# First loads, norm vectors, and four instruction orders in a two-layer transformer trunk: eight start-up loads in place of twelve

## The chip, the cores and the metric

The kernel runs on one core of one Trainium2 chip. Its time is device microseconds (us) of one launch, from the runs of the unprofiled kernel; lower is better. Everything else comes from one profiled execution. PE is TensorE (matmuls; its weight loads are shown as PEld), ACT is ScalarE, DVE is VectorE, POOL is GpSimd, and SP is the engine that issues most DMAs. A name with q (SPq) is an engine's sequencer.

## The reference

One sequence of 512 tokens with 1024 features goes through two layers, all in fp32. Cut to what matters:

```
for i in range(2):
    hn = rmsnorm(h, norm_mix_g[i])
    h = h + (even_mixer(hn) if i == 0 else odd_mixer(hn))   # projection, attention, output projection
    hn = rmsnorm(h, norm_mlp_g[i])
    h = h + square(relu(hn @ w_mlp_up[i])) @ w_mlp_down[i]   # 1024 -> 4096 -> 1024
    gate = sigmoid(rmsnorm(h, norm_ple_g[i]) @ w_ple_gate[i])
    h = h + (p[i] @ w_ple_proj[i]) * gate
return rmsnorm(h, final_norm_g)
```

Layer 0 mixes 8 stick-breaking heads with 4 differential heads, which need a scalar made of four short lambda vectors; layer 1 has 16 heads of dilated window attention. A relative-position bias table is added to the logits of all softmax heads.

## The kernel before

The state is held transposed: eight tiles h[0] to h[7], each 128 features by 512 tokens. Every fp32 operand of a matmul is split into a high part (ACT rounds it to fp32r: `hi`, `wh`) and the rest (DVE or POOL subtracts: `lo`, `wl`); a product is three matmuls, hi x wh, lo x wh and hi x wl (`mm3`, lines L141, L144, L145). The order on each engine is fixed when the program is built: a scheduler arranges the instructions by their dependencies, and `order(later, earlier)` adds a dependency by hand without a semaphore. Each engine then works strictly in its order. A DMA that SP issues is tied to one of eight completion semaphores in turn, so the ninth waits for the first to land.

Start-up. SP issues twelve loads: the norm vectors (`gcols`), and eight state tiles with the first weight block (the query weights of head group 2) in three pieces between them:

```
chunks = {0: slice(0, 2), 1: slice(2, 4), 3: slice(4, 8)}
nc.sync.dma_start(gcols, gvec)
for k in range(KT):
    nc.sync.dma_start(h[k], xT[k])
    if k in chunks:
        nc.sync.dma_start(raw0v[:, :, chunks[k]], src0[:, :, chunks[k]])
```

`raw0` holds the two output halves of the block one after the other, so that a piece of it has two rows per partition. Ten fp32 matmuls on an identity (`warm`, L311) come first on PE. Then the query product runs input tile by input tile (banks `sc`), then the key product (banks `mm`), half by half. `prepare()` (L337 to L359) loads the bias table's parts and the lambda vectors, and makes the bias rows (`urow`) and the lambda scalar (`neglam`). `statistics()` squares the eight state tiles on ACT (L248), adds them on DVE (L261), and `finish` turns the sum into 1/rms: split (L268, L269), two matmuls with a matrix of ones (L270, L271), Ln and Exp on ACT (L213, L216), and three DVE steps (L217 to L219) that give `rstd`. The evacuations of queries (`qq`, L493 to L500), keys (`kh`, `klz`, L509 to L511) and values (`v`, L461, L462) wait for it. The weight tiles `wh` and `wl` have three buffers each.

Attention. A step makes scores (L532, L533), a minimum and exponentials (L549, L552), transposes (L558) and their eviction (`transposed`, L566 and L567: `pth` on ACT, `ptl` on DVE), and later the product with the values (L577). `interleave` weaves these steps into the projection of the next group, or, for the last group, into the output projection `out_first`, which splits the finished head outputs `oT` (`split_tile`, L182, L183) as it needs them.

MLP. Up and down projections run in four chunks of the hidden width; the down product is a seven-product Strassen form on 256-column halves, with weight sums made on DVE (`s13`, `s24`, L797, L800) and split (L809, L810). In the last chunk the side sums are collected by accumulating DMAs from POOL (L835), and `finished(c)` folds them into h (`side_sums`, L920) and splits the new h for the gate projection.

End. `ple_final` turns h to token-major tiles of 128 tokens (`ht`), and for each makes the gate (L1032 to L1034), the sum of squares (L1035), 1/rms and the scaling (`finish`, L983 on ACT and L985 on DVE, then two output DMAs). The last tile uses Ln and Exp for 1/rms, the others an integer start with three Newton steps on DVE (`rsqrt_cols`, L284, L285, L279 to L281).

Of the kernel before, what the change touches and what calls it, by code (L numbers as in the profile page):

```python
# [19 lines left out]
P = 128  # L20
# [12 lines left out]
UL = 640  # L33
WARM = 10
# [28 lines left out]
def trunk(  # L63
    ctx: ExitStack,
    tc: tile.TileContext,
    xT, pT, gvec, t5_table, lambdas, w_in, w_outa, w_outb, w_up, w_down, w_gate, w_proj,
# [111 lines left out]
    def split_tile(src, scale=None, bufs=8):  # L178
        hi = apool.tile([P, S], F32R, tag="hi", name=nm("hi"), bufs=bufs)
        lo = apool.tile([P, S], F32R, tag="lo", name=nm("lo"), bufs=bufs)  # L180
        if scale is None:
            nc.scalar.activation(hi, src, AF.Copy)  # L182
            nc.vector.tensor_tensor(lo, src, hi.bitcast(F32), op=ALU.subtract)  # L183
        else:
            last_split[:] = [nc.scalar.activation(hi, src, AF.Copy, scale=scale).ins]
            nc.vector.scalar_tensor_tensor(lo, src, scale, hi.bitcast(F32), op0=ALU.mult, op1=ALU.subtract)  # L186
        return hi, lo
# [111 lines left out]
    h = [const([P, S], f"h{k}") for k in range(KT)]  # L299
    gcols = const([P, 49], "gcols")  # L300
# [13 lines left out]
    raw0v = raw0.rearrange("p (i k c) -> p i k c", i=2, k=KT)  # L314
    src0 = w_in[0, 0].rearrange("p (i k c) -> p i k c", i=2, k=KT)
    blk0 = [tuple(wpool.tile([P, KT, P], F32R, tag=t, name=nm(t), bufs=3) for t in ("wh", "wl")) for _ in range(2)]
    chunks = {0: slice(0, 2), 1: slice(2, 4), 3: slice(4, 8)}
    nc.sync.dma_start(gcols, gvec)
    for k in range(KT):
        nc.sync.dma_start(h[k], xT[k])  # L320
        if k in chunks:
            nc.sync.dma_start(raw0v[:, :, chunks[k]], src0[:, :, chunks[k]])
    for k in range(KT):
        norm.done(k, stats=False)
        if k in chunks:
            for i, (hi, lo) in enumerate(blk0):
                ck = chunks[k]
                nc.scalar.activation(hi[:, ck], raw0v[:, i, ck], AF.Copy)
                nc.vector.tensor_tensor(lo[:, ck], raw0v[:, i, ck], hi[:, ck].bitcast(F32), op=ALU.subtract)
# [4 lines left out]
    def prepare():  # L334
        a, b, c, d = (mix[0].tile([P, S], F32, tag="bias", name=nm("prep"), bufs=4) for _ in range(4))
        lamt = t2k("tmp")[:, 0:4 * HD].rearrange("p (j c) -> p j c", j=4)
# [9 lines left out]
        for c0, src, offm in ((0, a[0:32], (b[0:16], c[0:16])),  # L346
                              (512, d[0:32, 0:128], (d[0:16, 128:256], d[0:16, 256:384]))):
            up = ps("pv" if c0 == 0 else "tp")[0:16, 0:src.shape[-1]]
            nc.tensor.matmul(up, d[0:32, 384:400], src, start=True, stop=True)
            for l in range(2):  # L350
                nc.vector.scalar_tensor_tensor(offm[l], up, -1.0, offm[l], op0=ALU.mult, op1=ALU.add)
                nc.sync.dma_start(urow[l, :, c0:c0 + src.shape[-1]], offm[l])
        nc.vector.tensor_tensor(lamt[:, 0:2, :], lamt[:, 0:2, :], lamt[:, 2:4, :], op=ALU.mult)
        lsum = const([P, 2], "lsum")
        nc.vector.reduce_sum(lsum, lamt[:, 0:2, :], axis=AX.X)
        nc.scalar.activation(lsum, lsum, AF.Exp)
        nc.vector.tensor_tensor(neglam, lsum[:, 1:2], lsum[:, 0:1], op=ALU.subtract)
        nc.vector.tensor_scalar(neglam, neglam, -LAMBDA_INIT, None, op0=ALU.add)
        nc.vector.tensor_scalar(gsub, gcols[:, 48:49], -0.5 * (D // P) * (1.0 - LAMBDA_INIT), None, op0=ALU.mult)  # L359
# [31 lines left out]
    def mixer(layer, norm, nxt):  # L391
# [31 lines left out]
        first = []  # L423
# [3 lines left out]
        def project(g, cur):  # L427
# [38 lines left out]
            def queries_keys():  # L466
                qscale = -0.5 * HD ** -0.5 if kind == "sb" else 0.5 * HD ** -0.5
                qk, waiting = [], []
                for isq in (True, False):
                    src = next_block()  # L470
                    lo_eng[0] = nc.vector if start else nc.gpsimd
                    blk = blk0 if isq and start and not layer else block(src, KT, P)
                    lo_eng[0] = nc.gpsimd
# [87 lines left out]
        def transposed(tp, i, pt):  # L561
            n = P * (i + 1)
            src = tp[:, 0:n].rearrange("p (j c) -> p j c", c=P)
            dh = pth[pt][:, i:i + 3 * i + 1:3, :]
            dl = ptl[pt][:, i:i + 3 * i + 1:3, :]
            nc.scalar.activation(dh, src, AF.Copy)  # L566
            nc.vector.tensor_tensor(dl, src, dh.bitcast(F32), op=ALU.subtract)  # L567
# [116 lines left out]
        def out_first():  # L684
# [23 lines left out]
        else:  # L708
            interleave(out_first(), 72.0, attend(*cur))
# [20 lines left out]
    def mlp(layer, fpool, norm, nxt):  # L730
# [51 lines left out]
        def down(ch, c):  # L782
# [95 lines left out]
            if last and c:  # L878
                finished(c - 1)
# [28 lines left out]
        def finished(c):  # L908
            side_sums(c, low)
# [56 lines left out]
    def ple_final(layer, fpool, pj, norm):  # L966
# [13 lines left out]
        done = []  # L980

        def finish(t, r, after=()):
            cp = nc.scalar.activation(hk[t][:, 0:512], hk[t][:, 0:512], AF.Copy, scale=r)  # L983
            nc.sync.dma_start(out[0, t * P:(t + 1) * P, 0:512], hk[t][:, 0:512])
            sc = nc.vector.scalar_tensor_tensor(  # L985
                hk[t][:, 512:1024], hk[t][:, 512:1024], r, gb[:, 512:1024], op0=ALU.mult, op1=ALU.mult)
            if after:
                order(cp.ins, after[0].ins)
                order(sc.ins, after[1].ins)
            nc.sync.dma_start(out[0, t * P:(t + 1) * P, 512:1024], hk[t][:, 512:1024])  # L990

        for c in range(2):
# [31 lines left out]
            for t in range(QT):  # L1024
                last = c == 1 and t == QT - 1
                for i, (c0, n) in enumerate(parts[t]):
# [8 lines left out]
                    nc.scalar.activation(gt, hs, AF.Square, accum_out=ssq[t][:, c + i:c + i + 1])  # L1035
# [3 lines left out]
                m, r, w = (spool.tile([P, 1], F32, tag="fin", name=nm("fin"), bufs=6) for _ in range(3))  # L1039
                sq = ssq[t]  # L1040
                nc.vector.tensor_tensor(m, sq[:, 0:1], sq[:, 1:2], op=ALU.add)
                nc.vector.tensor_scalar(m, m, 1.0 / D, NORM_EPS, op0=ALU.mult, op1=ALU.add)
                if last:
                    tables = use_tables([sg.ins])
                    ln = nc.scalar.activation(r, sq[:, 2:3], AF.Ln, scale=1.0 / D, bias=m)
                    order(ln.ins, tables)
                    ex = nc.scalar.activation(r, r, AF.Exp, scale=-0.5)
                    nc.vector.scalar_tensor_tensor(m, sq[:, 2:3], 1.0 / D, m, op0=ALU.mult, op1=ALU.add)
                    newton(r, m, w)
                else:  # L1050
                    rsqrt_cols(r, m, w)
                done.append((t, r))
                if t < QT - 2:
                    finish(*done.pop())
        for t, r in done[::-1]:
            finish(t, r, () if t == QT - 1 else (ex, ad))
# [34 lines left out]
def _feeds(a):  # L1091
# [3 lines left out]
    for layer, w in enumerate((a["w_in_even"][0], a["w_in_odd"][0])):  # L1095
        blocks = []
        for j, g in enumerate(GROUPS[layer]):
# [6 lines left out]
            qk = [_pack(w, all8, c, 256, 2) for c in (q, k)]  # L1104
# [6 lines left out]
    gs = [a[n].reshape(DEPTH * KT, P) for n in ("norm_mix_g", "norm_mlp_g", "norm_ple_g")] + [a["subln_g"]]  # L1111
    onehot, offs = _consts()
    feeds = {
        "xT": a["x"][0].T.reshape(KT, P, S),
        "pT": a["p"][:, 0].transpose(0, 2, 1).reshape(DEPTH, 2, P, S),
        "gvec": np.concatenate(gs, axis=0).T,
# [39 lines left out]
```

## Time and profile before

| what | value |
|---|---|
| median of 3 runs | 1297.12 us (1297.03 to 1297.26) |
| the profiled execution: its own time, its span | 1296.47 us, 1294.7 us |
| PE busy, weight loads busy | 1277.1 us (99%), 1125.5 us (87%) |
| DVE, ACT, POOL busy | 1003.3 us (77%), 710.0 us (55%), 212.5 us (16%) |
| mean granted TensorE clock | 0.997 |
| DMA moved, mean rate | 144.25 MB, 111 GB/s |

The span runs from the first to the last instruction; the execution's own time is 1.8 us longer. Matmuls overlap in the record (a 512-column matmul is shown with 0.39 us, but the next starts 0.23 us later), so a PE that looks busy may still be waiting a few tenths; the start times of successive matmuls tell it.

### The profile page before, as it was taken

What the parts mean: (1) busy time and instruction counts of PE and PEld (TensorE: products, weight loads), DVE (VectorE), ACT (ScalarE), POOL (GpSimd) and SP (SyncE); (2) the same over time, 40 slices, a digit from 0 to 9 for tenths busy, and PEclk for the clock granted to TensorE, in tenths of its full rate; (3) what the DMA queues carried; (4) which work ended last, traced back from release to release, by engine and by line L of the source; (5) the groups of instructions that cost most, each with busy time, mean ns of one, the idle gap of its engine ahead of it and who ended that gap; (6) DMA issues with size and microseconds to landing.
All of it is one profiled execution on the core that took longest, in us unless ns stands there. A gap on an engine that the chain in (4) does not pass through costs nothing.

```text
span 1294.7 us, 19322 instructions
## 1 busy us (share of the span) xinstructions
PE 1277.1 (99%) x7520; PEld 1125.5 (87%) x7520; DVE 1003.3 (77%) x1673; ACT 710.0 (55%) x1149; POOL 212.5 (16%) x184
## 2 busy tenths in 40 slices
PE   9999999999999999999999999999999999999997
PEld 7988887888988989989889888788899898898986
DVE  6788798778858869679767777887785785986976
ACT  6667868555535334356456666765553443534544
POOL 2433433400000000001024333222000000000201
PEclk9999999999999999999999999999999999999998
DMA  6421423222232322647432222212323223255741
GB/s 213 141 82 53 160 74 114 90 98 98 85 112 98 101 99 95 195 110 201 153 128 84 82 90 77 70 58 83 112 98 103 93 98 121 75 153 141 185 165 66
DMA packets 33995, 144.25 MB, mean 111 GB/s; under 512 B 3888, under 2 KB 4624, under 8 KB 21232
## 3 DMA queue, kind: packets, MB, share of 16 engines
q1 hardware_dynamic: 29680, 135.16, 30.7%
q0 software_dynamic: 4224, 7.87, 3.5%
q8 instruction: 59, 0.97, 0.3%
q14 instruction: 32, 0.26, 0.1%
HBM read 131.92 MB, written 6.37 MB: 107 GB/s over the span
## 4 chain that ended last, share of the span: by engine, by line
PE 80%; DVE 10%; ACT 4%; DMA 2%; issue 2%; POOL 0%; SPq 0%; ACTq 0%; DVEq 0%; POOLq 0%
PE mm L141 11%; PE mm L144 11%; PE mm L145 11%; PE sc L144 5%; PE sc L145 5%; PE sc L141 5%; PE pv L145 4%; PE pv L144 4%; PE pv L141 4%; PE tp L145 4%; PE tp L144 4%; PE tp L141 4%; PE pv L577 3%; PE tp L558 2%; PE tp L894 2%
## 5 line engine op out<-in xcount | busy, mean ns | idle before, releaser
L122 ACT ACTIVATE wh<-raw 128x1024 fp32r<-128x1024 f32 (+1 forms) x156 | 160.5, 1034 | 135.4 <-PE mm L144 51.0
L126 POOL TENSOR_TENSOR wl<-raw,wh 128x512 fp32r<-128x512 f32 (+1 forms) x132 | 177.9, 1370 | 303.7 <-ACT wh L122 301.3
L141 PE MATMUL mm<-hi,wh 128*128 128x512 f32 x472 | 187.1, 396 | 0.2 <-ACT pjt L381 0.2
L145 PE MATMUL mm<-hi,wl 128*128 128x512 f32 x472 | 184.8, 391 | 0.1
L144 PE MATMUL mm<-lo,wh 128*128 128x512 f32 x472 | 184.6, 391 | 0.0
L128 DVE TENSOR_TENSOR wl<-raw,wh 128x1024 fp32r<-128x1024 f32 x90 | 109.6, 1222 | 39.6 <-ACT wh L122 34.1
L145 PEld LDWEIGHTS mm<-hi,wl 128*128 128x128 f32 x472 | 88.6, 188 | 20.0 <-POOL wl L126 0.5
L141 PEld LDWEIGHTS mm<-hi,wh 128*128 128x128 f32 x472 | 88.7, 188 | 16.9 <-ACT pjt L381 0.4
L144 PEld LDWEIGHTS mm<-lo,wh 128*128 128x128 f32 x472 | 88.8, 188 | 15.5
L780 POOL DMA_DIRECT2D s<-in_w_down_dram x4 | 4.5, 1123 | 580.0 <-DMA s<-in_w_down_dram 313.7
L809 ACT ACTIVATE wh<-s 128x1024 fp32r<-128x1024 f32 x58 | 61.1, 1053 | 53.0 <-DVE s L796 14.7
L552 ACT ACTIVATE e<-e,mn 128x128 f32<-128x128 f32 (+3 forms) x96 | 53.8, 561 | 62.3 <-DVE mn L549 61.9
L771 DVE TENSOR_TENSOR ul<-u,uh 128x1792 fp32r<-128x1792 f32 x32 | 64.8, 2024 | 29.6 <-ACT uh L770 29.5
L810 DVE TENSOR_TENSOR wl<-s,wh 128x1024 fp32r<-128x1024 f32 x58 | 70.8, 1221 | 12.6 <-ACT wh L809 12.2
L770 ACT ACTIVATE uh<-u 128x1792 fp32r<-128x1792 f32 x32 | 54.5, 1703 | 45.7 <-DVE u L768 45.4
L759 ACT ACTIVATE u<-u 128x512 f32<-128x512 f32 x64 | 39.7, 626 | 68.1 <-DVE u L758 68.1
L144 PE MATMUL sc<-lo,wh 128*128 128x512 f32 x184 | 72.3, 393 | 0.4 <-DVE lo L186 0.4
L141 PE MATMUL sc<-hi,wh 128*128 128x512 f32 x184 | 72.2, 392 | 0.0
L145 PE MATMUL sc<-hi,wl 128*128 128x512 f32 x184 | 71.9, 391 | 0.0
L141 PE MATMUL mm<-wh,hi 128*128 128x256 f32 (+1 forms) x216 | 63.4, 293 | 0.0
L145 PE MATMUL mm<-wh,lo 128*128 128x256 f32 (+1 forms) x216 | 63.0, 292 | 0.0
L144 PE MATMUL mm<-wl,hi 128*128 128x256 f32 (+1 forms) x216 | 62.9, 291 | 0.0
(305 smaller groups left out, 3885.8 us busy)
## 6 DMA issues: line engine op xcount, KB each, us to landing
raw<-in_w_up_dram SPq DMA_DIRECT2D x32, 1024.0 KB, 4.8
raw<-in_w_down_dram SPq DMA_DIRECT2D x32, 1024.0 KB, 4.9
raw<-in_w_in_dram SPq DMA_DIRECT2D x23, 1024.0 KB, 4.9
raw<-in_w_gate_dram SPq DMA_DIRECT2D x8, 1024.0 KB, 6.0
bias<-urow SPq DMA_DIRECT2D x24, 256.0 KB, 3.7
raw<-in_w_outa_dram SPq DMA_DIRECT2D x8, 768.0 KB, 4.2
pj<-pjd SPq DMA_DIRECT2D x16, 256.0 KB, 5.0
h<-in_xT_dram SPq DMA_DIRECT2D x8, 256.0 KB, 5.6
```

Of the source, the lines that this page charges most:

```text
L122: act = nc.scalar.activation(hi, src, AF.Copy)
L126: nc.gpsimd.tensor_tensor(lo[:, kx], src[:, kx], hi[:, kx].bitcast(F32), op=ALU.subtract)
L128: last_low[:] = [nc.vector.tensor_tensor(lo, src, hi.bitcast(F32), op=ALU.subtract).ins]
L141: mm = nc.tensor.matmul(acc, lh, rh, start=start, stop=False)
L144: nc.tensor.matmul(acc, lh, rl, start=False, stop=False)
L145: return mm.ins, nc.tensor.matmul(acc, ll, rh, start=False, stop=stop).ins
L552: nc.scalar.activation(e[:, 0:n], e[:, 0:n], AF.Exp, scale=-1.0, bias=mn, accum_out=s)
L759: chain.append(nc.scalar.activation(ui, ui, AF.Square, scale=0.5).ins)
L770: nc.scalar.activation(uh, u, AF.Copy)
L771: part = nc.vector.tensor_tensor(ul, u, uh.bitcast(F32), op=ALU.subtract)
L809: high[:] = [nc.scalar.activation(hi, src, AF.Copy).ins]
L810: low[:] = [nc.vector.tensor_tensor(lo, src, hi.bitcast(F32), op=ALU.subtract).ins]
```

## The change

The twelve first loads become eight: the norm vectors stand in the same rows as h[0] and come with it, h[1] to h[6] come in pairs, and the first weight block is laid out by input tile, so that each of its pieces is one run per partition. The splits of these loads are held in the order of the loads on ACT and DVE (`in_turn`). `prepare()` issues its loads before the first half of the key product, as it did, but its arithmetic (`rest`) follows behind that half. The squares of `statistics()` now stand behind the split of the key block instead of behind the splits of the state. Further: in layer 1's `out_first` all splits but the first are held behind the last eviction of the attention steps; in the last MLP chunk of both layers `finished(0)` is called one step later, inside c = 2 and behind that step's weight splits, and the product order of c = 2 is that of the others; and at the end the last tile's squares are summed on DVE, its 1/rms is made together with that of the tile before, and that tile's scaling follows behind it.

```
+    LOADS = (("h", 0, 1), ("w", 0, 2), ("h", 1, 3), ("w", 2, 4), ("h", 3, 5), ("w", 4, 8), ("h", 5, 7), ("h", 7, 8))
+    for what, a, b in LOADS:
+        if what == "h":
+            g = GPAD * (a == 0)                                  # GPAD = 64 columns of norm vectors
+            t = const([P, g + (b - a) * S], f"h{a}")
+            loads.append((t, xT[:, GPAD - g + a * S:GPAD + b * S]))
+            h += [t[:, g + j * S:g + (j + 1) * S] for j in range(b - a)]
+    gcols = loads[0][0][:, 0:GPAD]
...
-    raw0v = raw0.rearrange("p (i k c) -> p i k c", i=2, k=KT)
+    raw0v = raw0.rearrange("p (k i c) -> p i k c", i=2, k=KT)
+    for what, a, b in LOADS:
+        if what == "h":
+            nc.sync.dma_start(*loads.pop(0))
+        else:
+            cols = slice(a * 2 * P, b * 2 * P)
+            nc.sync.dma_start(raw0[:, cols], w_in[0, 0][:, cols])
+    def in_turn(act, sub):
+        for later, earlier in zip((act, sub), ahead):
+            order(later, earlier)
+        ahead[:] = [act, sub]
...
     def prepare():
-        lamt = t2k("tmp")[:, 0:4 * HD].rearrange("p (j c) -> p j c", j=4)
+        lamt = t2k("tmp2")[:, 0:4 * HD].rearrange("p (j c) -> p j c", j=4)
...
+        def rest():                    # the two matmuls on the bias table, urow, neglam, gsub
...
+        return rest
...
-                    norm.stats(k, last_split)
+                    norm.stats(k, first_high)          # last_high of the key block
...
-                    if start and not layer:
-                        prepare()
+                    rest = prepare() if start and not layer else None
                     for i, acc in enumerate(accs):
+                        if i and rest:
+                            rest()
                         yield from lin_units([acc], [blk[i]], ahl, 0, KT, False)
...
+            evicts[:] = [a.ins, nc.vector.tensor_tensor(dl, src, dh.bitcast(F32), op=ALU.subtract).ins]
...
-                        ohl.append(split_tile(oT[tiles[k]]))
+                        ohl.append(split_tile(oT[tiles[k]], behind=behind if k else ()))
...
-            interleave(out_first(), 72.0, attend(*cur))
+            interleave(out_first(list(evicts)), 72.0, attend(*cur))
...
             if last and c == 0:
                 lows.clear()
+            if last and c == 2:
+                finished(0, lows[-1:])
...
-                if last and c < 2:
+                if last:
                     product(1, 0, w13, 1, T3, True, False, ks)
                 product(0, 1, w24, 0, T2, False, True, ks)
-                if not last or c == 2:
+                if not last:
                     product(1, 0, w13, 1, T3, True, False, ks)
...
-            if last and c:
-                finished(c - 1)
+            if last and c == 2:
+                finished(1)
...
-                    nc.scalar.activation(gt, hs, AF.Square, accum_out=ssq[t][:, c + i:c + i + 1])
+                    if last:
+                        nc.vector.tensor_tensor_reduce(
+                            gt, hs, hs, op0=ALU.mult, op1=ALU.add, scale=1.0, scalar=0.0, accum_out=sq)
+                    else:
+                        nc.scalar.activation(gt, hs, AF.Square, accum_out=sq)
...
+                if t < QT - 2:
+                    rsqrt_cols(r[:, x], m[:, x], w[:, x])
+                    finish(t, r[:, x])
+                elif last:
                     tables = use_tables([sg.ins])
+                    ln = nc.scalar.activation(r[:, 0:1], m[:, 0:1], AF.Ln)
                     order(ln.ins, tables)
+                    nc.scalar.activation(r[:, 1:2], sq[:, 2:3], AF.Ln, scale=1.0 / D, bias=m[:, 1:2])
+                    nc.scalar.activation(r, r, AF.Exp, scale=-0.5)
...
+        for t in (QT - 1, QT - 2):
+            finish(t, r[:, t - 2:t - 1])
```

How the orders move, at the three places on which most rests. In the rows below h_93 to h_100 are the eight state tiles (after the change h_93 holds the norm vectors and h[0], h_94 holds h[1] and h[2], and so on). First ACT in the start-up, before: from the middle of the squares (L248) to the second half of the key block.

```order
L248 ACTIVATE e_335<-h_97 128x512
L122 ACTIVATE wh_259<-raw_257 128x1024
L248 ACTIVATE e_338<-h_98 128x512
L248 ACTIVATE e_341<-h_99 128x512
L248 ACTIVATE e_344<-h_100 128x512
L268 ACTIVATE e_348<-rstd_324 128x512
L356 ACTIVATE lsum<-lsum 128x2
L122 ACTIVATE wh_263<-raw_257 128x1024
```

And now, from the split of the last state tile on:

```order
L188 ACTIVATE hi_165<-h_97,h_93 128x512
L123 ACTIVATE wh_251<-raw_249 128x1024
L378 ACTIVATE lsum<-lsum 128x2
L123 ACTIVATE wh_255<-raw_249 128x1024
L252 ACTIVATE rstd_297<-h_93 128x512
L252 ACTIVATE e_299<-h_94 128x512
```

Both halves of the key block and the exponential of the lambda sums (lsum) now stand ahead of all eight squares. Further on in ACT's row, before, from a weight split (wh_645) amid the keys to the last of the first four value evictions (v):

```order
L122 ACTIVATE wh_645<-raw_546 128x1024
L509 ACTIVATE kh_412<-tmp_410 64x512
L510 ACTIVATE kh_412<-tmp_410 64x512
L509 ACTIVATE kh_416<-tmp_410 64x512
L510 ACTIVATE kh_416<-tmp_410 64x512
L461 ACTIVATE v_206<-pv_422,rcol_487 128x256 x2
L461 ACTIVATE v_206<-tp_423,rcol_487 128x256
L122 ACTIVATE wh_778<-raw_776 128x1024
L461 ACTIVATE v_206<-tp_423,rcol_487 128x256
```

And now, from the same weight split on:

```order
L123 ACTIVATE wh_637<-raw_538 128x1024
L536 ACTIVATE kh_351<-tmp_349 64x512
L537 ACTIVATE kh_351<-tmp_349 64x512
L536 ACTIVATE kh_355<-tmp_349 64x512
L537 ACTIVATE kh_355<-tmp_349 64x512
L485 ACTIVATE v_198<-pv_414,rcol_479 128x256
L536 ACTIVATE kh_404<-tmp_402 64x512
L537 ACTIVATE kh_404<-tmp_402 64x512
L536 ACTIVATE kh_408<-tmp_402 64x512
L537 ACTIVATE kh_408<-tmp_402 64x512
L485 ACTIVATE v_198<-pv_414,rcol_479 128x256
L485 ACTIVATE v_198<-tp_415,rcol_479 128x256
```

The weight split stands ahead of the keys instead of amid them, and the first value eviction ahead of the last four key evictions. Second, ACT in layer 1, where the evictions of the attention steps (pth) meet the splits of the head outputs (o), before:

```order
L566 ACTIVATE pth_6553<-tp_8597 128x3x128
L182 ACTIVATE hi_8663<-o_6560 128x512
L182 ACTIVATE hi_8673<-o_6561 128x512
L182 ACTIVATE hi_8683<-o_6562 128x512
L566 ACTIVATE pth_6553<-tp_8609 128x4x128
L182 ACTIVATE hi_8717<-o_6563 128x512
```

And now:

```order
L593 ACTIVATE pth_6545<-tp_8589 128x3x128
L183 ACTIVATE hi_8655<-o_6552 128x512
L593 ACTIVATE pth_6545<-tp_8601 128x4x128
L183 ACTIVATE hi_8665<-o_6553 128x512
L183 ACTIVATE hi_8675<-o_6554 128x512
```

The last eviction has moved ahead of two of the splits; DVE's order moves likewise. Third, DVE in the last MLP chunk of layer 1 (layer 0 reads the same), where the side sums of c = 0 (side, L920) meet the weights of c = 2 (s, wl), before:

```order
L920 TENSOR_TENSOR side_9340<-side_9340,side_9341 128x256
L797 TENSOR_TENSOR s_2182_12185<-s_2181_12184,raw_12182 128x512
L920 TENSOR_TENSOR h_93<-h_93,side_9340 128x256
L920 TENSOR_TENSOR side_9341<-side_9341,side_9340 128x256
L920 TENSOR_TENSOR h_93<-h_93,side_9340 128x256
L920 TENSOR_TENSOR h_94<-h_94,side_9341 128x256
L800 TENSOR_TENSOR s_2182_12185<-s_2182_12185,raw_12182 128x512
L920 TENSOR_TENSOR side_9341<-side_9341,side_9340 128x256
L186 SCALAR_TENSOR_TENSOR lo_12171<-h_93,gcols,hi_12170 128x512
L920 TENSOR_TENSOR h_94<-h_94,side_9341 128x256
L876 TENSOR_TENSOR h_95<-h_95,pv_12054 128x512
L810 TENSOR_TENSOR wl_12197<-s_2181_12184,wh_12196 128x1024
```

And now:

```order
L826 TENSOR_TENSOR s_2177_12157<-s_2176_12156,raw_12154 128x512
L839 TENSOR_TENSOR wl_12169<-s_2176_12156,wh_12168 128x1024
L829 TENSOR_TENSOR s_2177_12157<-s_2177_12157,raw_12154 128x512
L839 TENSOR_TENSOR e_12177<-raw_12154,e_12176 128x512
L839 TENSOR_TENSOR wl_12173<-s_2177_12157,wh_12172 128x1024
L907 TENSOR_TENSOR h_94<-h_94,pv_12046 128x512
L951 TENSOR_TENSOR h_93<-h_93,side_9333 128x256
```

The weight sums and their splits have moved ahead of every side sum of c = 0.

More of the change, by code (lines that the diff above doesn't have):

```diff
@@ L33 @@
 UL = 640
+GPAD = 64
 WARM = 10
@@ L176, in trunk, with split_tile @@
     last_split = []
-    def split_tile(src, scale=None, bufs=8):
+    def split_tile(src, scale=None, bufs=8, behind=()):
         hi = apool.tile([P, S], F32R, tag="hi", name=nm("hi"), bufs=bufs)
@@ L181, in split_tile @@
         if scale is None:
-            nc.scalar.activation(hi, src, AF.Copy)
-            nc.vector.tensor_tensor(lo, src, hi.bitcast(F32), op=ALU.subtract)
-        else:
-            last_split[:] = [nc.scalar.activation(hi, src, AF.Copy, scale=scale).ins]
-            nc.vector.scalar_tensor_tensor(lo, src, scale, hi.bitcast(F32), op0=ALU.mult, op1=ALU.subtract)
+            a = nc.scalar.activation(hi, src, AF.Copy)
+            b = nc.vector.tensor_tensor(lo, src, hi.bitcast(F32), op=ALU.subtract)
+            for later, earlier in zip((a, b), behind):
+                order(later.ins, earlier)
+        else:
+            a = nc.scalar.activation(hi, src, AF.Copy, scale=scale)
+            b = nc.vector.scalar_tensor_tensor(lo, src, scale, hi.bitcast(F32), op0=ALU.mult, op1=ALU.subtract)
+            last_split[:] = [a.ins, b.ins]
         return hi, lo
@@ L296, in tok_cols @@
         return rc
-    h = [const([P, S], f"h{k}") for k in range(KT)]
-    gcols = const([P, 49], "gcols")
+    LOADS = (("h", 0, 1), ("w", 0, 2), ("h", 1, 3), ("w", 2, 4), ("h", 3, 5), ("w", 4, 8), ("h", 5, 7), ("h", 7, 8))
+    h, loads = [], []
+    for what, a, b in LOADS:
[5 more added lines that the diff above has]
+    gcols = loads[0][0][:, 0:GPAD]
     gsub = const([P, 1], "gsub")
@@ L345, in prepare @@
         nc.sync.dma_start(lamt, bass.AP(tensor=lambdas.tensor, offset=lambdas.offset, ap=[[0, P], [HD, 4], [1, HD]]))
[L346 to L359, printed above, removed]
+        def rest():
+            for c0, src, offm in ((0, a[0:32], (b[0:16], c[0:16])),
+                                  (512, d[0:32, 0:128], (d[0:16, 128:256], d[0:16, 256:384]))):
+                up = ps("pv" if c0 == 0 else "tp")[0:16, 0:src.shape[-1]]
+                nc.tensor.matmul(up, d[0:32, 384:400], src, start=True, stop=True)
+                for l in range(2):
+                    nc.vector.scalar_tensor_tensor(offm[l], up, -1.0, offm[l], op0=ALU.mult, op1=ALU.add)
+                    nc.sync.dma_start(urow[l, :, c0:c0 + src.shape[-1]], offm[l])
+            nc.vector.tensor_tensor(lamt[:, 0:2, :], lamt[:, 0:2, :], lamt[:, 2:4, :], op=ALU.mult)
+            lsum = const([P, 2], "lsum")
+            nc.vector.reduce_sum(lsum, lamt[:, 0:2, :], axis=AX.X)
+            nc.scalar.activation(lsum, lsum, AF.Exp)
+            nc.vector.tensor_tensor(neglam, lsum[:, 1:2], lsum[:, 0:1], op=ALU.subtract)
+            nc.vector.tensor_scalar(neglam, neglam, -LAMBDA_INIT, None, op0=ALU.add)
+            nc.vector.tensor_scalar(gsub, gcols[:, 48:49], -0.5 * (D // P) * (1.0 - LAMBDA_INIT), None, op0=ALU.mult)
+        return rest
     pjd = dpool.tile([DEPTH, KT, P, S], F32, tag="pjd", name="pjd")
@@ L421, in next_block @@
             return w_in[layer, nblk[0] - 1]
-        first = []
+        first, first_high = [], []
         lead_in = ["sc", "sc", "mm", "mm", "pv", "tp"]
@@ L472, in queries_keys @@
                     blk = blk0 if isq and start and not layer else block(src, KT, P)
+                    if start and not isq:
+                        first_high[:] = last_high
                     lo_eng[0] = nc.gpsimd
@@ L682, in spread, with out_first @@
                 yield cost
-        def out_first():
+        def out_first(behind=()):
             for c in range(4):
@@ L1103, in _feeds @@
                 q, k, v = 1536 + 256 * (g - 2), 2048 + 256 * (g - 2), 2560 + 256 * (g - 2)
-            qk = [_pack(w, all8, c, 256, 2) for c in (q, k)]
+            qk = [_pack(w, all8, q, 256, 2 if layer or j else 1), _pack(w, all8, k, 256, 2)]
             vv = [_pack(w, all8, v, 256, 2, True)]
```

68 lines of the change are left out of this document (27 added, 41 removed).

## The prediction

> **What bounds the kernel now.** I read the page first, then TensorE's waits, then the chain that ended last, and last the timelines of the places that the diff touches. The page's first part and the summary of its chain (share of the span by engine):
>
> ```profile
> PE 1277.1 (99%) x7520; PEld 1125.5 (87%) x7520; DVE 1003.3 (77%) x1673; ACT 710.0 (55%) x1149; POOL 212.5 (16%) x184
> ...
> PE 80%; DVE 10%; ACT 4%; DMA 2%; issue 2%; POOL 0%; SPq 0%; ACTq 0%; DVEq 0%; POOLq 0%
> ```
>
> PE is the bound, and the change takes no product away: what it can win is PE's idle time, and what lies before its first and behind its last product. The largest waits of PE (total us, times, longest):
>
> ```profile
> PE mm L311 <- POOL ident masks.py:199: 1.5, 1, 1.5
> PE pv L577 <- ACT pth L566: 1.3, 1, 1.3
> ...
> PE mm L145 <- DVE wl L810: 0.7, 2, 0.4
> ```
>
> They are few and short, so the whole stake is some microseconds of 1294.7. The second and third stand in code that the diff reorders. I take the four parts in the order of the span.
>
> **The start-up, PE's side.** PE's timeline (start, duration), the chain's row for the last weight piece, and DMA in two stretches (last columns: clock, DMA share, GB/s):
>
> ```profile
> 1.47 4.63 PE L311 MATMUL mm<-ident 128*128 128x128 f32 x20 [1.47 <-POOL ident masks.py:199]
> 5.91 0.79 PE L141 MATMUL sc<-hi,wh 128*128 128x512 f32 x1
> ...
> 12.76 0.50 PE L141 MATMUL sc<-hi,wh 128*128 128x512 f32 x1
> 13.62 0.51 PE L144 MATMUL sc<-lo,wh 128*128 128x512 f32 x1 [0.35 <-DVE lo L186]
> ...
> 18.74 0.39 PE L145 MATMUL sc<-hi,wl 128*128 128x512 f32 x1
> ```
>
> ```profile
> 4.70 6.22 DMA raw<-in_w_in_dram
> ```
>
> ```profile
> 3.00:8.00 5.00, 5.00 (x22) 4.53 (x21) 1.94 (x4) 2.62 (x6) 1.45 (x6) 1.00 0.85 263
> 8.00:13.00 5.00, 4.94 (x20) 3.22 (x18) 4.08 (x10) 3.70 (x7) 0.00 (x0) 1.00 1.05 386
> ```
>
> The first product cannot start before the warm-up ends at about 5.9, so earlier first loads win nothing there. From 5.91 to 18.97 (18.74 and one pitch of 0.23) PE does 48 matmuls, which at 0.23 take 11.04: 2.0 are lost, some 0.7 of it in the slow first products and 1.3 in waits for splits, the largest 0.63 (12.76 to 13.62, less 0.23). All of them follow late loads; the chain names the last weight piece, 6.22 us in flight. The bytes in flight bound what fewer, longer loads can win: at 386 GB/s from the third microsecond on, 8.00 would see 1.93 MB instead of 1.31, and the rest come 1.6 us sooner. If the early rate stays, nothing is won. I take 1.3 to 1.4, all the waits, since 1.6 exceeds them; below, 0.
>
> **The start-up, the chain behind it.** The statistics do not follow as fast. Rows of DVE, ACT and POOL, then of the chain (start, duration), and PE's next stall:
>
> ```profile
> 17.06 1.04 ACT L122 ACTIVATE wh<-raw 128x1024 fp32r<-128x1024 f32 x1
> 22.06 0.63 ACT L268 ACTIVATE e<-rstd 128x512 fp32r<-128x512 f32 x1 [2.40 <-DVE rstd L261]
> ```
>
> ```profile
> 19.75 2.28 DVE L261 TENSOR_TENSOR rstd<-rstd,e 128x512 f32<-128x512 f32 x3
> ```
>
> ```profile
> 34.12 3.00 POOL L126 TENSOR_TENSOR wl<-raw,wh 128x512 fp32r<-128x512 f32 x2 [3.75 <-ACT wh L122]
> ```
>
> ```profile
> 26.91 0.58 ACT rstd L213
> ...
> 31.67 0.64 ACT qq L499
> ...
> 35.16 0.80 DVE qq L500
> 35.99 1.68 DVE qq L500
> ...
> 41.11 1.06 ACT wh L122
> ...
> 44.11 1.68 DVE klz L511
> 45.82 0.50 DVE v L462
> ```
>
> ```profile
> 59.16 0.36 PE L532 MATMUL sc<-kh,qq 128*128 128x256 f32 x1 [0.50 <-DVE mn L549]
> ```
>
> Before, the adds of the squares end at 22.03. After, both halves of the key block stand ahead of the squares. The second half needs the weight buffer that the query product frees at its end, 18.97 less 1.4, about 17.5. Its split (1.04), its subtraction on DVE, then seven adds at 0.76 (2.28 for three) end at about 24.7; the split of the sum and PE's two matmuls bring Ln to about 27.0, where it was 26.91. PE waits some 0.8 at the first of those matmuls, which now stands earlier in its row. So of PE's 1.4 about 0.7 are left when it reaches the values, and the chain starts no earlier.
>
> The chain itself then runs ACT and DVE in turns to the stall at 59.16. In it the weight split at 41.11 stood amid the keys; it now stands ahead of the first key, where ACT waits for DVE: 1.06 less some issue, -0.9. The first value eviction is moved ahead of the last four keys, off the path: -0.5 (the row at 45.82). Against this, another weight split now stands ahead of the first qq and needs the buffer that the key product frees at about 31.1; it ends at about 32.1, past 31.67: +0.5. Ln gives +0.1. Net -0.8. PE, 0.7 earlier at the values, can follow that, and a chain that does better also shortens the stall (0.50). I take -1.0, the -0.8 and some of the stall; the best is the whole -1.4 and most of the stall, -1.8; the worst +0.5, if Ln waits for the later adds and the blocked steps below get dearer.
>
> The rows that are long are those beside POOL's: qq took 1.68 at 35.99 where the one ahead of it took 0.80, and POOL worked from 34.12 to 37.12; klz took 1.68 at 44.11. After the change POOL's pieces start with their weight splits, 1 to 2 us sooner for the first and some 4 for the second, so other DVE steps meet them; I count no gain from this. The Trainium skill, "SBUF — State Buffer", section "Who interferes with whom", has it that a DVE instruction with two SBUF inputs and a GpSimd instruction that reads SBUF exclude each other. By that rule too the block moves and does not vanish; if instead DVE met no POOL piece at all, two steps would be shorter by 0.9 each, the part would be worth -1.8, and the sum would give 1294.0 in place of the 1294.8 below.
>
> The loads of `prepare` move too. Its SP issue and, from the DMA view of the first 20 us, its time to landing:
>
> ```profile
> 13.58 0.35 SPq L345 DMA_DIRECT2D tmp<-in_lambdas_dram  x1
> ```
>
> ```profile
> tmp<-in_lambdas_dram SPq DMA_DIRECT2D x1, 128.0 KB, 4.4
> ```
>
> It landed at about 18.0. Four issues fewer ahead of it on SP bring it to 15.5 to 16.5. Its two DVE steps and lsum now stand ahead of the second key split on ACT (wanted at 17.5) and of the squares, so this load must be there by about 16.9. It is hidden if it is.
>
> **Layer 1's output projection.** ACT, then PE:
>
> ```profile
> 834.59 1.67 ACT L182 ACTIVATE hi<-o 128x512 fp32r<-128x512 f32 x3
> 836.17 0.58 ACT L566 ACTIVATE pth<-tp 128x512 fp32r<-128x512 f32 x1
> ```
>
> ```profile
> 836.80 0.49 PE L577 MATMUL pv<-pth,v 128*128 128x512 f32 x1 [1.29 <-ACT pth L566]
> 837.81 0.50 PE L577 MATMUL pv<-ptl,v 128*128 128x512 f32 x1 [0.52 <-DVE ptl L567]
> ```
>
> The eviction stood behind three splits of 0.56 (1.67 for three) and now behind one; the value products start 1.1 us sooner, and the 0.52 shrinks. But the same splits, on ACT and DVE, are then still to be done, and what follows on DVE (the queries and keys of the steps behind) comes only some 0.5 sooner. PE depends on DVE again within fifteen microseconds. I take -0.5: between -0.2 (most is given back) and -1.3 (all of the first wait).
>
> **MLP, c = 2, in both layers.** PE, then DVE, of layer 1:
>
> ```profile
> 1214.95 0.28 PE L144 MATMUL sc<-ul,wh 128*128 128x256 f32 x1
> 1215.61 0.39 PE L145 MATMUL mm<-uh,wl 128*128 128x256 f32 x1 [0.38 <-DVE wl L810]
> ```
>
> ```profile
> 1209.18 0.42 DVE L920 TENSOR_TENSOR h<-h,side 128x256 f32<-128x256 f32 x1 [0.67 <-DMA side<-u]
> ...
> 1214.34 1.22 DVE L810 TENSOR_TENSOR wl<-s,wh 128x1024 fp32r<-128x1024 f32 x1
> ```
>
> DVE waits for a side DMA at 1209.18, and 5 us of its steps later comes the `wl` that PE lacks at 1215.07 (1214.95 and a pitch of 0.12): 0.54, and 0.11 for the slow restart, 0.65 in a layer. With the side sums behind the weights this wait goes: -1.3 for two layers. The eight sums do not vanish; their next reader is the split for the gate, which has until the last projection. If it stalls there, half comes back: -0.6.
>
> **The end.** DVE's last Newton step of the tile before the last and ACT's Ln, in the chain; then SP's output issues; then DMA (last two columns):
>
> ```profile
> 1287.18 0.16 DVE fin L281
> ...
> 1288.71 0.30 ACT fin L1045
> ```
>
> ```profile
> 1289.88 1.12 SPq L984 DMA_DIRECT2D out_dram<-ht  x2
> ```
>
> ```profile
> 1289.00:1290.00 1.00, 0.00 (x0) 0.00 (x0) 0.78 (x5) 0.91 (x4) 0.00 (x0) 0.50 0.36 135
> 1292.00:1293.00 1.00, 0.00 (x0) 0.00 (x0) 0.00 (x0) 0.00 (x0) 0.00 (x0) 0.50 0.90 342
> ```
>
> Without the Newton steps in between, the last tile's 1/rms is ready some 0.8 sooner. But the tile before now waits for it too: its piece that went out at 1288.82, filling 1289 to 1290 with 0.135 MB, joins the other three at about 1289.8. At 342 GB/s those 0.135 MB cost 0.4 at the end. I take +0.5, from -0.2 (the issues decide and start a little sooner) to +1.0 (a whole 256 KB piece later and the scalings two deep).
>
> **The sum.** -1.0 - 0.5 - 1.3 + 0.5 = -2.3: the profiled execution's own 1296.47 (its span and 1.8 around it) becomes 1294.2. The median of the runs, 1297.12, stands 0.65 above that execution, so what is to be compared with it is 1294.8.
>
> **Rivals.** *All waits go.* Start-up -1.4, output projection -1.3, MLP -1.3, end 0: -4.0, 1293.1. For it: each stall names one releaser, and each is moved. Against it: behind each the same engine has the same work to do. *The start-up gives nothing*, because the chain from Ln to 59.16 decides and Ln is no earlier; the loads may even land as before, since the DMA share was 0.85 already from 3 to 8. Then -0.5 - 1.3 + 0.5: 1295.8. *Slower: the lambda load.* If it lands later than about 16.9, lsum holds the key block's second half, the squares and PE, one for one. The start-up's gain is gone from 17.9 and the kernel is slower from 19.2 (16.9 and 2.3), by 0.2% (2.6) from about 21.8. For it: its flight was 4.4 us among other loads, and the later ones in the rank waited for earlier ones to land. Against it: four issues of about 0.6 fewer stand ahead of it. With a landing between 20 and 22 it gives 1298 to 1300.
>
> **How the numbers follow.** The forecast has 0.45, all waits gone 0.25, no gain at the start 0.2, slower 0.1. The forecast's own range is 1294.0 to 1295.7; to hold 8 in 10, the range goes from all waits gone and most of the stall at 59.16 (1293.1 - 0.4 = 1292.7) to nothing at the start, the MLP giving half back and the dear end of the tail (1295.8 + 0.7 + 0.5 = 1297.0). A change under 0.2%, 2.6 us, is about what a measurement of this kernel cannot tell from none, so faster means below 1294.5: all waits gone, 0.25, and of the forecast's 0.45 the 0.14 that lie between 1294.0 and 1294.5, 0.39 in all. Slower means above 1299.7, the dearer part of the lambda case: 0.06. The rest, 0.55, is within.
>
> **What would show it.** In the changed trace: the query product's last matmul at about 17.3 instead of 18.74, with no pitch above 0.4 behind 8 us; a PE wait of 0.5 to 1 at the first matmul on the split sum; Ln at about 27; no weight split amid the keys; the stall at 59 at half its size or gone. The wait for pth in layer 1 below 0.4, but the values' products less than 1 sooner ten microseconds later. No PE wait for a strip of `wl` in c = 2. Four output issues close together near 1290, and a last landing no sooner behind the last product than now. Wrong it would be if PE waits in the first 20 us for lsum's successors, if the side sums hold PE in the last chunk, or if the output DMAs of the two last tiles finish well sooner or later than reckoned.

## The result, and the profile after

The changed kernel takes 1300.55 us (median of 13 runs, 1298.63 to 1301.59), the kernel before 1297.12 on the same chip; the ratio is 1.0025, with a 95% interval of 1.0018 to 1.0033. It is 3.4 us slower, where 1294.8 was predicted and the range ended at 1297.0. The profiled execution has a span of 1298.6 us. On its page, PE's work is as it was, and its share fell by a point:

```profile
span 1298.6 us, 19304 instructions
...
PE 1278.5 (98%) x7520; PEld 1126.3 (87%) x7520; DVE 1003.6 (77%) x1666; ACT 709.8 (55%) x1146; POOL 213.7 (16%) x184
...
PE 84%; DVE 8%; ACT 4%; DMA 2%; issue 2%; SPq 0%; POOL 0%; DVEq 0%; ACTq 0%; POOLq 0%
```

PE's waits tell where to look. The two that headed the list of code that the diff touches (pth and the `wl` of c = 2) are gone from its head, and a new one is larger than both:

```profile
PE tp L274 <- ACT e L272: 2.7, 1, 2.7
PE mm L322 <- POOL ident masks.py:199: 1.5, 1, 1.5
...
PE pv L606 <- DVE ptl L594: 0.3, 1, 0.3
```

L274 is the first matmul on the split sum of squares. ACT and DVE ahead of it (start, duration):

```profile
17.56 1.06 ACT L123 ACTIVATE wh<-raw 128x1024 fp32r<-128x1024 f32 x1 [2.45 <-DMA raw<-in_w_in_dram]
20.43 0.20 ACT L378 ACTIVATE lsum<-lsum 128x2 f32<-128x2 f32 x1 [1.81 <-DVE lsum L377]
20.54 1.04 ACT L123 ACTIVATE wh<-raw 128x1024 fp32r<-128x1024 f32 x1
21.49 0.61 ACT L252 ACTIVATE rstd<-h 128x512 f32<-128x512 f32 x1
22.01 3.74 ACT L252 ACTIVATE e<-h 128x512 f32<-128x512 f32 x7
...
29.13 0.63 ACT L272 ACTIVATE e<-rstd 128x512 fp32r<-128x512 f32 x1 [1.48 <-DVE rstd L265]
31.70 0.69 ACT L217 ACTIVATE rstd<-tp,eps_n 128x512 f32<-128x512 f32 x1 [1.95 <-PE tp L275]
```

```profile
18.65 1.23 DVE L129 TENSOR_TENSOR wl<-raw,wh 128x1024 fp32r<-128x1024 f32 x1 [2.66 <-ACT wh L123]
19.79 0.28 DVE L375 TENSOR_TENSOR tmp<-tmp 128x128 f32<-128x128 f32 x1
20.11 0.29 DVE L377 TENSOR_REDUCE lsum<-tmp 128x2 f32<-128x128 f32 x1
...
22.76 6.33 DVE L265 TENSOR_TENSOR rstd<-rstd,e 128x512 f32<-128x512 f32 x7
```

ACT sits idle twice, 2.45 us for the key block's load and 1.81 us for lsum, and only then come the second key split and all eight squares, which before filled just such time. DVE's lambda steps stand behind the subtraction of the first key half. The adds end at 29.1, where they ended at 22.0. PE, and the granted clock (the column behind the five engines), in and behind the wait:

```profile
26.71 0.39 PE L146 MATMUL mm<-hi,wl 128*128 128x512 f32 x1
29.81 0.49 PE L274 MATMUL tp<-e,ones_r 128*128 128x512 f32 x1 [2.71 <-ACT e L272]
...
31.89 0.63 PE L142 MATMUL mm<-hi,wh 128*128 128x512 f32 x1
32.31 0.63 PE L145 MATMUL mm<-lo,wh 128*128 128x512 f32 x1
```

```profile
29.80:34.40 4.60, 4.59 (x13) 3.35 (x14) 3.25 (x6) 1.32 (x2) 3.35 (x3) 0.65 0.23 30
```

Behind the wait the clock is 0.65 for 4.6 us and the matmuls come every 0.43 us instead of 0.23. The wait (2.9 in start times) and the slow matmuls (1.6) make most of PE's delay; at the second set of scores (L559) it is 5.8 us late (55.04, where it was 49.27). The later parts give 2.0 of that back, in steps read from the starts of the same matmul in both traces: 5.8 to 4.8 in the MLP of layer 0, from 4.9 to 3.9 and back to 4.6 at the output projection of layer 1, from 4.5 to 3.8 over the MLP of layer 1.

At the end the last 1/rms is indeed ready sooner behind the last product (DVE's last step at 1292.48, 3.7 us behind it, where it was 4.6). The four issues and the DMA (last two columns) show what that brings:

```profile
1293.48 0.33 SPq L1014 DMA_DIRECT2D out_dram<-ht  x1
1293.91 0.38 SPq L1017 DMA_DIRECT2D out_dram<-ht  x1
1294.38 0.40 SPq L1014 DMA_DIRECT2D out_dram<-ht  x1
1294.88 0.40 SPq L1017 DMA_DIRECT2D out_dram<-ht  x1
```

```profile
1293.00:1294.00 1.00, 0.00 (x0) 0.00 (x0) 1.00 (x2) 1.00 (x2) 0.00 (x0) 1.00 0.00 0
...
1296.00:1297.00 1.00, 0.00 (x0) 0.00 (x0) 0.00 (x0) 0.00 (x0) 0.00 (x0) 0.50 1.03 389
```

The DMA engines are idle until 1294 and then full: the span ends 9.8 us behind the last product, where it ended 9.7 behind it.

### The profile page after: what moved, and what is told of

Read it like the earlier page. It is cut to its first block, busy times and chain, and to the rows that moved or that the text cites. A ratio compares the mean times of both kernels' runs of the same rounds, so it can differ in the third digit from the quotient of the medians.

```text
span 1298.6 us, 19304 instructions
## 1 busy us (share of the span) xinstructions
PE 1278.5 (98%) x7520; PEld 1126.3 (87%) x7520; DVE 1003.6 (77%) x1666; ACT 709.8 (55%) x1146; POOL 213.7 (16%) x184
## 4 chain that ended last, share of the span: by engine, by line
PE 84%; DVE 8%; ACT 4%; DMA 2%; issue 2%; SPq 0%; POOL 0%; DVEq 0%; ACTq 0%; POOLq 0%
PE mm L142 11%; PE mm L145 11%; PE mm L146 11%; PE sc L145 5%; PE sc L146 5%; PE sc L142 5%; PE pv L146 5%; PE pv L145 5%; PE pv L142 4%; PE tp L146 4%; PE tp L145 4%; PE tp L142 4%; PE pv L606 3%; PE tp L585 2%; PE tp L925 2%
```

## The experiments

The theory after the result: the new order of the start-up costs the time (squares and lsum behind the key block). The rival: the loads do, since the key block's split began at 17.56 instead of 17.06. The medians below are of 5 to 12 runs, those of the kernel before of 27 to 33 on the same chip. Differences in us are of medians; the ratio with its 95% interval is taken over the runs, and can differ from that of the two medians by up to 0.0007 (0.9 us).

| kernel | us | before | ratio (interval) |
|---|---|---|---|
| eight loads only | 1296.79 | 1296.77 | 0.9993 (0.9982 to 1.0005) |
| both start-up orders only | 1302.61 | 1296.77 | 1.0050 (1.0036 to 1.0063) |
| changed, squares back | 1294.91 | 1296.77 | 0.9990 (0.9981 to 0.9999) |
| changed, lambda late | 1298.45 | 1296.77 | 1.0015 (1.0006 to 1.0024) |
| three later parts only | 1295.03 | 1296.91 | 0.9987 (0.9978 to 0.9996) |
| output projection only | 1296.23 | 1296.91 | 0.9997 (0.9988 to 1.0006) |
| MLP only | 1295.61 | 1296.91 | 0.9991 (0.9982 to 1.0000) |
| end only | 1297.16 | 1296.91 | 1.0000 (0.9991 to 1.0009) |
| output projection and MLP | 1294.88 | 1296.62 | 0.9985 (0.9976 to 0.9994) |
| squares' place only | 1304.98 | 1296.62 | 1.0066 (1.0053 to 1.0079) |
| prepare's place only | 1296.74 | 1296.62 | 1.0003 (0.9995 to 1.0012) |
| changed, PE kept busy | 1298.71 | 1296.62 | 1.0017 (1.0009 to 1.0026) |

**Eight loads only.** The kernel before with the new loads, the new weight layout and `in_turn`:

```
+    for what, a, b in LOADS:
+        if what == "h":
+            nc.sync.dma_start(*loads.pop(0))
...
-                    norm.stats(k, last_split)
+                    norm.stats(k, last_split[:1])
```

> The kernel before with only the eight loads and the weight layout by input tile; squares, lambda and all later parts as before. Theory (the new order of the statistics costs the time, the loads do not): the stall of PE at the split sum stays away, PE reaches the stall near 59 us within 1 us of before, total 1296.3 to 1297.8 us. Rival (the merged loads land late, the key block at 17.5 instead of 16.65, and that costs the time): PE is some 3 us or more later near 60 us, total 1300 or more.

1296.79 us, no change. PE is within 0.8 us of before from 14 us on. The rival falls: the loads cost nothing measurable, though the key block came late here too (it landed at 17.4; ACT's split began at 17.87, behind four squares). Nor is a gain clear of none (the interval allows up to 2.3). And the late landing is not theirs alone: it was 16.7 with eight loads in "squares back" and 17.6 with twelve in "three later parts only".

**Both orders only.** The kernel before, with its twelve loads:

```
-                    norm.stats(k, last_split)
+                    norm.stats(k, first_high)
...
                     for i, acc in enumerate(accs):
+                        if i and rest:
+                            rest()
```

> The kernel before, with its twelve loads, and only the two moves of order in the start-up: squares behind the key block's split, arithmetic of prepare behind the first half of the key product. Theory (order): PE waits 2 to 3 us for the split sum and runs slower right after it; total 1300.5 to 1303 us, since nothing of the later parts gives back. Rival (loads): no such wait, total 1296.5 to 1298.

1302.61 us, 5.8 slower, with the same wait as the changed kernel:

```profile
PE tp L273 <- ACT e L271: 2.7, 1, 2.7
```

The clock behind it is 0.64 over 4.6 us. The theory's numbers came, all of the loss and no gain.

**Squares back.** The changed kernel with

```
-                    norm.stats(k, first_high)
+                    norm.stats(k, last_split[:1])
```

> The changed kernel with one edit: the squares stand behind the splits of the state again, not behind the key block. Theory (order): the 2.7 us wait for the split sum falls below 0.5 and the whole gain of the later parts shows, total 1294.5 to 1296 us. Rival (loads): the key block still lands at 17.5 and holds the chain, total 1298 or more.

1294.91 us, and no wait for the split sum: five squares stand ahead of the first key split, and ACT works without a gap from the state's splits to the last square. The 2.40 that it then waits for the adds it waited in the kernel before, too.

```profile
14.48 0.62 ACT L252 ACTIVATE rstd<-h 128x512 f32<-128x512 f32 x1
15.00 2.18 ACT L252 ACTIVATE e<-h 128x512 f32<-128x512 f32 x4
17.09 1.05 ACT L123 ACTIVATE wh<-raw 128x1024 fp32r<-128x1024 f32 x1
18.04 1.66 ACT L252 ACTIVATE e<-h 128x512 f32<-128x512 f32 x3
22.09 0.63 ACT L272 ACTIVATE e<-rstd 128x512 fp32r<-128x512 f32 x1 [2.40 <-DVE rstd L265]
```

One line of the diff thus turns 3.4 us slower into 1.9 faster. `rest` and the loads are still in this kernel; the line is what costs. It moves more than the squares: lsum (22.64) and the second key split (22.73) also stand behind the split of the sum again, as they did before. PE waits 1.0 us for the first key half's subtraction here, and the clock stays at 1.00.

**Lambda late.** The changed kernel, squares still behind the key block, with the lambda arithmetic called behind the statistics:

```
+            order(mul.ins, sums[0])      # behind the split of the sum
...
+            order(ex.ins, root[0])       # lsum behind the Exp of 1/rms
```

> The changed kernel with the lambda arithmetic moved behind the statistics; squares stay behind the key block. Tells how much of the loss is lsum standing ahead of the key block's second half (rival D of the prediction) and how much the squares standing behind both halves. If lsum decides: the second key split starts at 19.1 instead of 20.5 and the wait for the split sum is gone, total 1296 to 1297. If the squares' place decides: the wait shrinks by the 1.4 only, about 1.3 us left, and the total is 1298 to 1299.5.

1298.45 us: within the second case. The wait for the split sum is 1.1 instead of 2.7, and the clock falls behind it all the same:

```profile
PE tp L274 <- ACT e L272: 1.1, 1, 1.1
```

```profile
28.40:33.00 4.60, 4.60 (x13) 3.32 (x14) 4.43 (x8) 1.41 (x3) 3.38 (x3) 0.63 0.17 27
```

lsum's place accounts for some 1.8 of the 5.3 us that lie between the changed kernel and the one with the squares back (+3.4 to +1.7 against each one's kernel before); the squares' place for the other 3.5. The two intervals overlap, so by the times alone lsum's part is not clear of nothing; PE's lateness at the second set of scores, 4.3 instead of 5.8, gives it 1.4.

**The later parts.** The kernel before with all three, and with each alone: output projection, MLP, end.

```
-            interleave(out_first(), 72.0, attend(*cur))
+            interleave(out_first(list(evicts)), 72.0, attend(*cur))
...
+            if last and c == 2:
+                finished(0, lows[-1:])
...
-        for t, r in done[::-1]:
-            finish(t, r, () if t == QT - 1 else (ex, ad))
+        for t in (QT - 1, QT - 2):
+            finish(t, r[:, t - 2:t - 1])
```

> The kernel before with the three later parts alone (output projection of layer 1, MLP c = 2, the end); start-up as before. From the offsets between the two traces: -0.7 to -1.1 for the output projection, -1.2 for the MLP, +0.1 for the end: 1295.0 to 1295.6 us. If the later parts won only because PE was late when it reached them, 1296.5 to 1297.

> The kernel before with only the splits of layer 1's output projection held behind the last eviction. By the prediction -0.5 (1296.6); by the offsets of the two traces -0.7; by the rival that the first wait goes whole, -1.3 (1295.8).

> The kernel before with only the later side sums in the MLP's third chunk, both layers. By the prediction -1.3 (1295.8); if the side sums stall PE in the last chunk, -0.6 (1296.5).

> The kernel before with only the new end. By the prediction +0.5 (1297.6): the last scaling is ready 0.9 sooner, four output transfers come together. By the offsets of the two traces +0.1 (1297.2). If the issues decided, -0.2 (1296.9).

All three: 1295.03, -1.9. Alone: -0.7, -1.3 and +0.25, together -1.7. Of these four only the three together are clear of no change; the intervals of the output projection and of the end include it, and that of the MLP ends at it. So none of the later parts caused the loss, and they gain as much with the old start-up as with the new.

**Output projection and MLP.** The first two of these edits without the third:

> The kernel before with the two parts that gained alone (output projection of layer 1, MLP c = 2); start-up and end as before. From the single runs, -0.7 and -1.3: 1294.8 to 1295.1 us, about the same as with the new end, or 0.25 less. If the parts overlap, 1295.5.

1294.88 us (0.9985, 0.9976 to 0.9994), the shortest of all, and no different from the three parts together (1295.03) or the changed kernel with its squares back (1294.91).

**Squares' place only, prepare's place only.** The kernel before with one of the two start-up orders each, the first and the second edit of "both orders only":

> The kernel before with only the squares behind the key block's split; the loads and the arithmetic of prepare stand in the program as before. If the squares' place is the whole cause, the slow-down of the two moves together is all here: +5 to +6 us, 1302 to 1303. If the place of prepare's matmuls and DVE steps among the statistics has a large share, +2 to +4. The clock right behind the PE wait tells whether prepare's small matmuls ahead of the wait had to do with its fall to 0.65: it stays at 1.0 here if they had.

> The kernel before with only the arithmetic of prepare behind the first half of the key product. If it is harmless by itself, within 0.5 us of before; if it costs by itself (its matmuls between the split sum and the rest), +1 to +3 us.

The second did nothing measurable (1296.74). The first missed its expectation upwards: 1304.98, 8.4 us slower, more than both moves together. PE waits 5.1 us, because the seven adds take 9.07 us on DVE beside POOL, which now works through four weight pieces at the same time:

```profile
PE tp L273 <- ACT e L271: 5.1, 1, 5.1
```

```profile
23.80 9.07 DVE L264 TENSOR_TENSOR rstd<-rstd,e 128x512 f32<-128x512 f32 x7
```

```profile
25.19 6.33 POOL L126 TENSOR_TENSOR wl<-raw,wh 128x512 fp32r<-128x512 f32 x4 [20.69 <-ACT wh L122]
```

```profile
33.60:39.70 6.10, 6.10 (x14) 4.78 (x15) 3.17 (x5) 1.32 (x2) 0.00 (x0) 0.50 0.84 317
```

An add by itself takes 0.69 us, here as before; the four that meet POOL's pieces take 1.56 to 1.66. The clock behind the wait is 0.50 for 6.1 us, though for 7 us ahead of it stood dense products and no small ones: behind a wait of this length it falls without the small matmuls of `prepare`. Prepare's new place, harmless alone, takes 2.5 us off this loss (5.8 with it, 8.4 without). Without it prepare's DVE steps (22.21 to 23.88) stand ahead of the adds, which begin at 23.80 instead of the 22.42 of "both orders only", while POOL begins at 25.19 instead of 26.43: so four adds meet POOL instead of one.

**PE kept busy.** The changed kernel with 16 idle-time matmuls in the wait, and `rest` ahead of the statistics:

```
+            for x in range(16 * len(fill)):
+                mm = nc.tensor.matmul(mp, ones_r, fill[0], start=True, stop=True)
...
+                            if rest:
+                                rest()
                             statistics()
```

> The changed kernel with 16 more matmuls (on a state tile and the ones, into the bank that the split sum then overwrites) in the PE wait for the split sum, and prepare's arithmetic just ahead of the statistics instead of behind. They add 3.6 us of PE work to a wait of 2.9 and make nothing faster by themselves. If PE's idleness lowers the granted clock (0.65 for 4.6 us behind the wait, 1.6 us lost), the clock stays above 0.95 and the total is 1299 to 1300.5 us. If the clock falls for another reason, it stays near 0.65 and the total is 1301 to 1302.5.

1298.71 us, a little under the range given for the first case, and 1.3 less over its kernel before than the changed kernel is (+2.1 to +3.4). The fill, and the clock behind it:

```profile
25.97 4.01 PE L275 MATMUL tp<-hi,ones_r 128*128 128x512 f32 x16
```

```profile
30.50:35.00 4.50, 3.98 (x17) 3.30 (x18) 2.45 (x4) 1.33 (x2) 2.87 (x2) 1.00 0.17 28
```

The clock stays at 1.00, with a last wait of 0.97 us inside. So the clock's fall goes with the wait: with matmuls in it there is none. The edit also took prepare's last two small matmuls from behind the split sum to ahead of the wait, and whether they had a share in the fall behind the shorter waits is not shown. How much of the 1.3 is the clock is not separated: the weight split ahead of the first qq went back to its old place in this kernel too.

## Why the prediction was wrong

**The start-up, PE's side: wrong in size.** The query product was to end 1.4 sooner. Its last matmul starts at 18.86 (18.74 before); in the five profiled kernels with eight loads it starts between 18.06 and 19.55, in the nine with twelve between 18.50 and 19.26. The step that failed is the bound "at 386 GB/s from the third microsecond on". Between 3 and 8 us the new loads move 251 GB/s, the old 263; only from 8 on are they faster:

```profile
3.00:8.00 5.00, 5.00 (x21) 4.35 (x20) 1.67 (x4) 1.45 (x3) 1.46 (x6) 1.00 0.87 251
8.00:13.00 5.00, 4.14 (x18) 2.96 (x17) 4.02 (x9) 4.38 (x8) 0.00 (x0) 1.00 1.04 422
```

And a load of two tiles lands as one: h[1] and h[2] are both there only when ACT starts on them at 8.05, where h[1] alone was split at 6.82.

```profile
8.05 1.33 ACT L188 ACTIVATE hi<-h,h 128x512 fp32r<-128x512 f32 x2 [1.79 <-DMA h<-in_xT_dram]
```

The likeliest value was taken at the far end of its own bound; its near end, 0, is what the loads alone brought, as far as the times tell.

**The start-up, the chain: the step that decided, mis-sized by 6 us.** The mechanism was named (the second key split, its subtraction and seven adds behind it, then PE waiting at the split sum). The sizes were not. The second split was to start at 17.5, when its weight buffer came free, and started at 20.54. Of these 3.0 us, 1.1 are ACT's own: it split the first half until 18.62, since that load landed at 17.53. The other 1.9 are lsum, which stood ahead. From 17.5 the terms named (1.04, a subtraction of 1.2, seven adds of 0.76) add up to 25.1 and not to 24.7. And the last add met POOL's first weight piece, which begins when the weight splits do (26.78), and took more than twice its time:

```profile
26.73 0.70 DVE rstd L265
27.53 1.58 DVE rstd L265
```

The end of the adds, 24.7, became 29.1; PE's wait, 0.8, became 2.7; and the slower clock behind it, which the prediction left out, cost 1.6 more. Ln came at 31.70 instead of 27.0, and the rest followed: the weight split ahead of the first qq, priced at +0.5, waited for a key product that ended 6 us later than reckoned and started at 37.24. The predicted -1.0 for the whole start-up was +5.3: the changed kernel's +3.4 less the -1.9 of the other parts.

**The rival "lambda load" had the right queue and the wrong releaser.** It was told by its landing: harmless if there by 16.9, worth 0.2% from 21.8. Its landing was 18.8 (issued at 13.81, 5.0 in flight), not 15.5 to 16.5: four issues fewer did not bring it forward, as SP's issues of `prepare` still came one by one up to 13.81, most of them after a wait for one of the first loads to land.

```profile
10.57 1.59 SPq L361 DMA_DIRECT2D prep<-in_offs_dram  x2
13.14 0.33 SPq L362 DMA_DIRECT2D prep<-in_offs_dram  x1
13.81 0.35 SPq L365 DMA_DIRECT2D tmp<-in_lambdas_dram  x1
```

But even that was not what lsum waited for. DVE's multiply stood behind the subtraction of the first key half (18.65 to 19.8), which waits for the key block, and DVE works in order. By these rows lsum would have come at 20.4 even with the load there at 16. The prediction looked at the operand and not at the instruction ahead in DVE's row; taking lsum out was worth 1.8 us by the medians, 1.4 by the traces.

**POOL's block.** That it "moves and does not vanish" was right, and the Trainium skill's rule ("SBUF — State Buffer", "Who interferes with whom") agrees with what the traces show: 0.69 for an add by itself, 1.56 to 1.66 for one that met a piece of POOL's. The error was to count no loss from where it moved to, a chain of adds that PE waits for.

**The later parts: as forecast, but clear of noise only together.** MLP -1.3 predicted and -1.3 measured, though its interval (0.9982 to 1.0000) allows from nothing to -2.3; no wait for `wl` of c = 2 is left. Output projection -0.5, measured -0.7 and not clear of nothing; its trace shows the give-back as argued, on the first matmul that waits for DVE's tmp behind the value products:

```profile
840.69 0.51 PE L606 MATMUL pv<-pth,v 128*128 128x512 f32 x1 [0.24 <-ACT pth L593]
841.54 0.50 PE L606 MATMUL pv<-ptl,v 128*128 128x512 f32 x1 [0.34 <-DVE ptl L594]
...
843.94 0.50 PE L142 MATMUL mm<-hi,wh 128*128 128x512 f32 x1 [0.39 <-DVE tmp L520]
```

The give-back goes on behind these rows: with this part alone PE gains 1.0 at 836 us and keeps 0.3 of it at 850. The end +0.5, measured +0.25 and not clear of nothing. Its price was read off half of the piece: in the trace before, the 256 KB filled 1289.5 to 1290.5 (262 GB/s over that microsecond), and the stretch read, 1289 to 1290, holds only the first 0.135 MB. The near agreement says little. The sum of these three, -1.3, against -1.9 measured: with the start-up left alone the range would have held.

## What to carry to other kernels

Work that is moved "behind" something on an in-order engine inherits every wait of that something and of all that stands between: read the new row of each engine and ask, for each instruction in it, what the one ahead of it waits for, before asking when its own operand lands. Squares that filled ACT's and DVE's idle time while a weight load was in flight cost nothing there; put behind that load they became the chain that PE waits for. And price a new PE wait at more than its length where the clock falls behind it, as it did here.

## What the runs showed of the hardware

The granted clock fell after short waits. A wait of 1.1 us in the start-up was followed by 0.63 over 4.6 us, one of 2.7 by 0.65 over 4.6, one of 5.1 by 0.50 over 6.1; with the wait filled by matmuls it stayed at 1.00. The means over 4.6 us mix two states. In slices of 1 us the changed kernel's clock is 1.00 until 31, 1.2 us after the wait ended, and then half:

```profile
31.00:32.00 1.00, 1.00 (x5) 0.77 (x4) 0.77 (x3) 0.30 (x1) 1.00 (x2) 0.60 0.02 8
32.00:33.00 1.00, 1.00 (x4) 0.81 (x3) 0.00 (x0) 0.97 (x2) 1.00 (x1) 0.50 0.00 0
33.00:34.00 1.00, 1.00 (x3) 0.74 (x3) 0.88 (x2) 0.06 (x1) 0.15 (x1) 0.50 0.00 0
34.00:35.00 1.00, 1.00 (x5) 0.81 (x4) 0.97 (x2) 0.00 (x0) 0.00 (x0) 0.69 0.90 106
```

Read as time at one half, that is 3.4 us. The same sum gives 3.4 behind the waits of "both orders only" (2.7) and "lambda late" (1.1), and 6.8, twice as much, around that of "squares' place only" (5.1), where the clock fell while PE still waited. So in these four kernels the loss of speed had the length 3.4 or its double, whatever the wait.

The Trainium skill, "TensorE: Matmul & The Clock Gate", section "Part 1: The HAM clock gate (the "warmup" mystery)", gives half the clock after at least one idle window of about 3.4 us: the 0.50 of these slices agrees with half; the length of the idleness does not, since 1.1 us was enough. It is not always enough: in layer 1 of the kernel before, a wait of 1.3 us (the 1.45 below, with hardly a matmul running) left the clock at 1.00.

```profile
835.35:836.80 1.45, 0.16 (x1) 0.00 (x0) 1.45 (x3) 1.45 (x4) 0.00 (x0) 1.00 0.27 110
836.80:841.00 4.20, 3.68 (x17) 2.84 (x18) 3.50 (x6) 3.11 (x6) 2.21 (x2) 1.00 0.00 0
```

What tells the two apart stays open; no run here varied it. One difference is that small matmuls of `prepare` stand on both sides of the wait of 1.1 us (25.30 and 28.80), and none beside that in layer 1.
